# A second planner for the order of each engine: backward by the ends found, forward by the latest times, seven rounds

## The chip, the cores and the metric

The kernel runs on one core of a Trainium2 chip. The metric is the device time of one execution in microseconds. The engines are PE (TensorE, the matmul engine), DVE (VectorE), ACT (ScalarE), POOL (GpSimd) and SP, whose queue issues all DMAs of this kernel.

## What is computed

One inference step of a two-layer streaming encoder for 1152 rows of width 1024 (1024 prompt rows, 8 x 16 sample rows), in float32. The reference, cut to one layer:

```
def _layer(x, l, W, mem_k, mem_v, conv_hist, lat_past, kr_past, start):
    h = _rmsnorm(x, W['norm_mix_g'][l]) @ W['w_in'][l]
    a_u, a_v, b_a, b_g, c_q, c_kv, c_kr = jnp.split(h, cuts, axis=-1)
    y_a, v_rows = _gmlp(a_u, a_v, ...)              # spatial gating in chunks of 128 rows
    y_b, conv_state = _conv_module(b_a, b_g, ...)   # GLU, depthwise convolution of width 31, LayerNorm, swish
    # latent attention: 8 heads, keys and values from a 128-wide latent, QK-norm, rotary part, block-causal mask
    y_c = _mla_attend(q_nope, q_rope, pos, k_nope, kr_all, v, kpos)
    x = x + jnp.concatenate([y_a, y_b, y_c], axis=-1) @ W['w_out'][l]
    # cross-attention into 256 memory tokens, 4 heads of 128, QK-norm
    x = x + om @ W['w_mo'][l]
    x = x + jnp.square(jax.nn.relu(_rmsnorm(x, W['norm_ffn_g'][l]) @ W['w_ff1'][l])) @ W['w_ff2'][l]
```

## The kernel before

The rows lie in three chunks of 384 (`CW`), features on the partitions. Most operands are kept as a high and a low part in fp32r (`halves`, `split`, `split_scaled`), and one product is three matmuls (`mm3`). Two large SBUF areas, `arena_f` (float32) and `arena_r` (fp32r), are cut into buffers by an allocator, and eight PSUM banks are handed round. Weights come by DMA as raw float32, are split by ACT and DVE, and wait in a queue for the matmuls.

A layer runs through five stages: `mixer_in` (input projections; `conv` with 31 passes on DVE for each of two channel tiles, and `taps`, the same convolution for the sample rows as adds on POOL), `attention` (token projections, norms, scores, values) together with `mix` (gating), `mixer_out` (output projection, part of it `early`), `cross`, and `ffn`. In attention each tile of tokens needs a scale: sums of squares on ACT, an add on DVE, a power on POOL (`small_rstd`), then ACT again.

The program is not written in the order in which it runs. Threads (Python generators) emit instructions, and a first planner, `plan`, picks the thread that goes on, by priority and by a model of when each engine is free. This fixes every instruction, its engine, its buffer and its bank, and `log` keeps the planned start of each in `trace`; `real` holds a cost for each (a table of formulas in `mm`, `ptt`, `stt` and the like, as n x 2.1 + 147 ns for an add on POOL). Then `fix_order` works out for each instruction which others it must follow (data, buffers reused, banks reused, order of activation tables), and `in_order` runs a list scheduler over that graph: each engine, and the one DMA queue, takes from what is ready the instruction with the least key. The order that comes out is written into the program as an order for each engine. Between engines `BEHIND` is added: 200 ns after PE, 150 after ACT and DVE, 120 after POOL, 1900 after a DMA. `array` is the planner's model of PE's clock, and `in_order` also charges POOL and DVE for holding one another up.

The key in question is line 420: the planned start, less `URGE` (0.05) times `rest`, the longest chain of costs behind the instruction.

Of the kernel before, what the change touches and what calls it, by code (L numbers as in the profile page):

```python
# [68 lines left out]

TICK = 10240.0 / 3  # L70
WARM = 3060
URGE = 0.05

BEHIND = {"PE": 200.0, "ACT": 150.0, "DVE": 150.0, "POOL": 120.0, "DMA": 1900.0}

# [173 lines left out]
def span(ap, dims, rows):  # L249

    t = ap.tensor
    off, size = ap.offset, sum((n - 1) * abs(s) for s, n in dims) + 1
    if dims[0][0] == math.prod(list(t.shape)[1:]):
        s, n = dims[0]
        size -= (n - 1) * s
        return t.name, off // s, off // s + n, off % s, off % s + size
    if rows:
        s, n = dims[0]
        size -= (n - 1) * s
        return f"{t.name} {off // (s * n)}", 0, 128, off % s, off % s + size  # L260
    return t.name, 0, 128, off, off + size
# [11 lines left out]
class Enc:  # L273
# [39 lines left out]
    def array(self, t, cost, cols):  # L313


        c0 = cols / cost
        if t < self.tick * TICK:
            self.tick, self.cols_out = 0, 0.0
        while True:
            i = int(t // TICK)  # L320
            if i > self.tick:
                self.warm = i == self.tick + 1 and self.cols_out >= WARM
                self.tick, self.cols_out = i, 0.0
            f = 1.0 if self.warm else 2.0
            d = min(cost * f, (i + 1) * TICK - t)
            cost -= d / f
            self.cols_out += c0 * d / f
            if cost < 1e-6:
                return t + d
            t = (i + 1) * TICK + 1e-6  # L330
# [23 lines left out]
    def fix_order(self):  # L354


        n = len(self.trace)
        index = {ins.name: i for i, (_, ins) in enumerate(self.trace)}
        preds = [set() for _ in range(n)]
        for a, b in self.manual:  # L360
            preds[index[a]].add(index[b])
        seen, banks = {}, {b.tensor.name: {} for b in self.banks}
        rows = (self.xscr.tensor.name, self.yscr.tensor.name, self.hscr.tensor.name)
        for i, (_, ins) in enumerate(self.trace):
            new = []
            for write, aps in ((False, ins.ins), (True, ins.outs)):
                for x in aps:
                    ap = getattr(x, "bass_ap", None)
                    if ap is not None and not isinstance(ap.tensor, bass.DRamTensorHandle):
                        new.append((write,) + span(ap, x.ap, ap.tensor.name in rows))  # L370
            for name in {x[1] for x in new if x[1] in banks}:
                used = banks[name]
                preds[i].update(used.values())
                used[ins.engine] = i
            for write, name, p0, p1, lo, hi in new:
                cells = seen.setdefault(name, {})
                for c in range(lo // 128, (hi + 127) // 128):
                    keep = []
                    for e in cells.get(c, ()):
                        j, w, q0, q1, a, b = e  # L380
                        hit = a < hi and lo < b and q0 < p1 and p0 < q1
                        if hit and (w or write) and j != i:
                            preds[i].add(j)
                        a, b = max(a, c * 128), min(b, c * 128 + 128)
                        if not (write and j != i and lo <= a and b <= hi and p0 <= q0 and q1 <= p1):
                            keep.append(e)
                    keep.append((i, write, p0, p1, lo, hi))
                    cells[c] = keep
        prev = {}
        for i in self.in_order(preds):  # L390
            ins = self.trace[i][1]
            if ins.engine in prev:
                self._after(ins, prev[ins.engine])
            prev[ins.engine] = ins
# [9 lines left out]
                k += self.n(ap) > 1  # L404
        return k > 1 or isinstance(ins, mybir.InstTensorCopy)

    def in_order(self, preds):
        n = len(self.trace)
        succ, left, ready = [[] for _ in range(n)], [len(p) for p in preds], [0.0] * n
        for i, p in enumerate(preds):  # L410
            for j in p:
                succ[j].append(i)
        engs = {r[0] for r in self.real}
        rest = [0.0] * n
        for i in reversed(range(n)):
            e = self.real[i][0]
            rest[i] += self.real[i][1]
            for j in preds[i]:
                rest[j] = max(rest[j], rest[i] + (0.0 if e == "PE" == self.real[j][0] else BEHIND[self.real[j][0]]))
        key = [t - URGE * r for (t, _), r in zip(self.trace, rest)]  # L420
        soon, now, free = {e: [] for e in engs}, {e: [] for e in engs}, {e: 0.0 for e in engs}
        columns, narrow, last, out = {}, False, {"DVE": [], "POOL": []}, []
        for i in range(n):
            if not left[i]:
                heapq.heappush(soon[self.real[i][0]], (0.0, i))
        while len(out) < n:
            t, e = min((free[e] if now[e] else max(free[e], soon[e][0][0]), e) for e in engs if now[e] or soon[e])
            while soon[e] and soon[e][0][0] <= t:
                i = heapq.heappop(soon[e])[1]
                heapq.heappush(now[e], (key[i], i))  # L430
            i = None
            if e == "PE" and narrow:
                more = [x for x in now[e] if self.real[x[1]][3]]
                if more:
                    i = min(more)
                    now[e].remove(i)
                    heapq.heapify(now[e])
            _, i = i or heapq.heappop(now[e])
            _, cost, cols, tile = self.real[i]
            if e == "PE":  # L440
                if bool(tile) != narrow:
                    t, narrow = t + 92.0, not narrow
                if tile:
                    cs = range(*tile, 32)
                    t = max([t] + [columns.get(c, 0.0) for c in cs])
                    free[e] = self.array(t, 30.0, cols)
                    end = t + cost * (1.0 if self.warm else 2.0)
                    for c in cs:
                        columns[c] = end
                else:  # L450
                    t = max([t] + list(columns.values()))
                    columns = {}
                    end = free[e] = self.array(t, cost, cols)
            else:
                end = t + cost
                if e == "POOL" or e == "DVE" and self.holds(self.trace[i][1]):
                    for a, b in last["DVE" if e == "POOL" else "POOL"][-12:]:
                        if a <= t < b:
                            end = max(end, b + cost - (60.0 if e == "POOL" else 160.0))
                    last[e].append((t, end))  # L460
                free[e] = end
            out.append(i)
            for j in succ[i]:
                left[j] -= 1
                if e != "PE" or self.real[j][0] != "PE":
                    ready[j] = max(ready[j], end + BEHIND[e])
                if not left[j]:
                    heapq.heappush(soon[self.real[j][0]], (ready[j], j))
        return out

    def _after(self, a, b):
        self.tc.add_manual_dep(
# [33 lines left out]
    def set(self, *name, t=None):  # L506
        self.events[name] = self.last() if t is None else t
# [2351 lines left out]
```

## Time and profile before

| | us |
|---|---|
| median of 3 runs | 3009.69 (3009.36 to 3010.79) |
| the profiled execution | 3009.8 |
| its span, first to last instruction | 3008.0 |
| PE busy | 2920.9 (97%) |
| DVE busy | 2118.2 (70%) |
| ACT busy | 1417.4 (47%) |
| POOL busy | 357.1 (12%) |
| mean granted clock of PE | 0.979 |

Busy time is the union of an engine's instructions. Matmuls overlap, so the mean of one is longer than its share of the busy time. The granted clock is the share of 2.4 GHz that PE was given, as a mean over a stretch; it has two levels, 1.2 and 2.4 GHz. DMAs wait in SP's queue in their order; such waits are told apart from busy time.

### The profile page before, as it was taken

Reading aid. Unit: us, or ns where it says so; the run is one execution under the profiler, and the core shown is the slowest. Engines: PE = TensorE matmul, PEld = TensorE weight load, DVE = VectorE, ACT = ScalarE, POOL = GpSimd, SP = SyncE. Lnnn points to the kernel's source line nnn. Section 1 sums busy time; section 2 is a strip of 40 time slices with the busy share of each in tenths; the row PEclk is TensorE's granted clock in tenths of the full one; section 3 lists DMA queues with packets and bytes.
Section 4 is the critical chain, followed back from the end, with each engine's and each line's share of the span. In section 5 each row is a group of like instructions: output and inputs, shape, how many; then the busy total and the mean of one; then the engine's idle time right before and its main releaser. Section 6 shows DMA issues by size and latency. Waiting matters only on the chain.

```text
span 3008.0 us, 52427 instructions
## 1 busy us (share of the span) xinstructions
PE 2920.9 (97%) x19708; PEld 2807.8 (93%) x19708; DVE 2118.2 (70%) x4568; ACT 1417.4 (47%) x3762; POOL 357.1 (12%) x427
## 2 busy tenths in 40 slices
PE   8989999999999999999999789999999999999999
PEld 8988988979999999999999688989799999999999
DVE  8986767668655577677898867676687555777775
ACT  7566775466544452111364666664665444521110
POOL 0743220000000000000044422120100000000000
PEclk9989998999999999999999889999999999999999
DMA  6302215433232254222333010453333323532221
GB/s 208 113 30 79 66 45 166 153 120 120 101 125 95 106 185 126 90 90 76 111 99 96 26 36 28 136 182 124 123 113 125 110 91 119 181 121 90 90 73 64
DMA packets 156110, 318.14 MB, mean 106 GB/s; under 512 B 22864, under 2 KB 79824, under 8 KB 155600
## 3 DMA queue, kind: packets, MB, share of 16 engines
q1 hardware_dynamic: 155856, 314.79, 31.4%
q8 instruction: 155, 2.54, 0.3%
q14 instruction: 99, 0.81, 0.1%
HBM read 225.94 MB, written 88.80 MB: 105 GB/s over the span
## 4 chain that ended last, share of the span: by engine, by line
PE 87%; DVE 6%; ACT 4%; POOL 1%; issue 1%; DMA 0%; SPq 0%; DVEq 0%; POOLq 0%; ACTq 0%
PE bank L707 84%; PE bank L730 3%; ACT arena_f L589 3%; DVE arena_f L679 1%; POOL arena_f L614 1%; DVE arena_f L610 1%; DVE arena_r L610 1%; DVE arena_f L683 1%; DVE arena_r L679 1%; ACT arena_r L589 1%; ACT L582 0%; DVE arena_r L750 0%; ACT arena_r L606 0%; DVE arena_f L671 0%; DVE bank L691 0%
## 5 line engine op out<-in xcount | busy, mean ns | idle before, releaser
L707 PE MATMUL bank<-arena_r 128*128 128x384 f32 (+7 forms) x16464 | 2671.5, 321 | 38.8 <-DVE arena_r L750 9.3
L707 PEld LDWEIGHTS bank<-arena_r 128*128 128x128 f32 (+2 forms) x16464 | 2539.8, 190 | 103.8 <-ACT arena_f L589 21.2
L610 DVE TENSOR_TENSOR arena_f<-arena_f,bank 128x384 f32<-128x384 f32 (+1 forms) x1286 | 667.3, 529 | 409.9 <-PE bank L707 404.5
L606 ACT CAST arena_r<-arena_f 128x512 fp32r<-128x512 f32 (+5 forms) x547 | 387.8, 729 | 866.9 <-PE bank L707 799.2
L610 DVE TENSOR_TENSOR arena_r<-arena_f,arena_r 128x512 fp32r<-128x512 f32 (+7 forms) x608 | 496.3, 827 | 148.9 <-PE bank L707 124.3
L589 ACT ACTIVATE arena_f<-arena_f 128x384 f32<-128x384 f32 (+5 forms) x628 | 374.8, 620 | 230.0 <-DVE arena_f L610 171.4
L614 POOL TENSOR_TENSOR arena_f<-arena_f 128x128 f32<-128x128 f32 (+6 forms) x298 | 327.3, 1106 | 837.0 <-DVE arena_f L610 284.6
L589 ACT ACTIVATE arena_f<-bank,arena_f 128x64 f32<-128x64 f32 (+7 forms) x774 | 272.6, 424 | 202.1 <-PE bank L707 68.7
L610 DVE TENSOR_TENSOR arena_f<-arena_f 128x384 f32<-128x384 f32 (+11 forms) x832 | 299.0, 371 | 71.5 <-ACT arena_f L589 62.8
L589 ACT ACTIVATE arena_f<-bank 128x64 f32<-128x64 f32 (+6 forms) x682 | 207.7, 349 | 82.6 <-PE bank L707 44.0
L707 PE MATMUL bank<-arena_f 128*128 128x65 f32 (+7 forms) x2344 | 228.4, 290 | 11.1 <-issue 7.9
L679 DVE SCALAR_TENSOR_TENSOR arena_f<-arena_f 128x1024 f32<-128x1024 f32 (+3 forms) x236 | 221.2, 949 | 3.9 <-POOL arena_f L614 1.6
L707 PEld LDWEIGHTS bank<-arena_f 128*128 128x128 f32 (+2 forms) x2344 | 188.1, 158 | 30.7 <-issue 14.0
L730 PE MATMUL bank<-arena_f 128*128 128x128 f32 (+2 forms) x900 | 162.3, 287 | 33.4 <-ACT arena_f L589 23.8
L730 PEld LDWEIGHTS bank<-arena_f 128*128 128x128 f32 (+2 forms) x900 | 111.7, 142 | 61.4 <-ACT arena_f L589 31.4
L695 POOL MEMSET arena_f<- 128x8 f32 (+3 forms) x125 | 30.6, 251 | 973.5 <-DVE arena_r L610 760.7
L606 ACT COPY arena_f<-bank 128x288 f32<-128x288 f32 (+4 forms) x272 | 104.7, 387 | 76.0 <-PE bank L707 62.4
L683 DVE TENSOR_REDUCE arena_f<-bank 128x1 f32<-128x512 f32 (+4 forms) x224 | 119.4, 555 | 10.2 <-PE bank L707 9.5
L589 ACT ACTIVATION_READ_ACCUMULATOR arena_f<-bank 128x1 f32 x396 | 94.1, 275 | 0.0
L610 DVE TENSOR_TENSOR arena_r<-bank,arena_r 128x256 fp32r<-128x256 f32 (+3 forms) x114 | 57.8, 511 | 34.6 <-ACT arena_r L606 33.6
L679 DVE SCALAR_TENSOR_TENSOR arena_r<-bank,arena_f,arena_r 100x512 fp32r<-100x512 f32 (+3 forms) x92 | 65.9, 725 | 17.9 <-ACT arena_r L589 17.2
L589 ACT ACTIVATE arena_r<-bank,arena_f 100x512 fp32r<-100x512 f32 (+3 forms) x92 | 61.7, 690 | 28.6 <-PE bank L730 28.3
(24 smaller groups left out, 538.6 us busy)
## 6 DMA issues: line engine op xcount, KB each, us to landing
arena_f<-w SPq DMA_DIRECT2D x140, 512.0 KB, 3.6
hscr<-arena_f SPq DMA_DIRECT2D x64, 576.0 KB, 3.2
arena_f<-hscr SPq DMA_DIRECT2D x96, 384.0 KB, 3.6
xscr<-arena_f SPq DMA_DIRECT2D x96, 192.0 KB, 1.9
arena_f<-xscr SPq DMA_DIRECT2D x48, 384.0 KB, 4.1
arena_f<-xscr SPq DMA_DIRECT2D x72, 192.0 KB, 2.5
xscr<-arena_f SPq DMA_DIRECT2D x36, 384.0 KB, 2.3
arena_f<-mkc SPq DMA_DIRECT2D x32, 256.0 KB, 3.1
```

What stands on the lines that cost most here:

```text
L589: i = self.nc.scalar.activation(out, in_, func, **kw)
L606: self.nc.scalar.copy(out, in_)
L610: self.nc.vector.tensor_tensor(out=out, in0=a, in1=b, op=op)
L614: self.nc.gpsimd.tensor_tensor(out=out, in0=a, in1=b, op=op)
L679: self.nc.vector.scalar_tensor_tensor(out, a, s, b, op0=o0, op1=o1)
L683: self.nc.vector.tensor_reduce(out, in_, axis=AX.X, op=op, **kw)
L695: self.nc.gpsimd.memset(ap, val)
L707: self.nc.tensor.matmul(out, a, b, start=start, stop=stop, **kw)
L730: self.nc.tensor.transpose(out, in_, self.ident)
```

## The change

`in_order` takes its key from outside, and gives back the order and the modelled end of every instruction. `best_order` calls it seven times. In the first round the key is the planned start alone. After each round `latest` runs a list scheduler backward over the same graph: from the last instruction to the first, each engine takes from what has no unplaced successor the one that ended last in the round before; the negative of the time so found is the latest start, and is the key of the next round. The order with the earliest modelled end of the seven is kept. `URGE` and `rest` go; the backward pass charges the plain costs (30 ns of PE for a matmul on a part of the array), without `array` and without the holding up of POOL and DVE. In `array` two lines go that set the clock model back when time went back; `in_order` now sets it back itself at its start.

```diff
--- before.py
+++ after.py
@@ -69,7 +69,7 @@
 
 TICK = 10240.0 / 3
 WARM = 3060
-URGE = 0.05
+ROUNDS = 7
 
 BEHIND = {"PE": 200.0, "ACT": 150.0, "DVE": 150.0, "POOL": 120.0, "DMA": 1900.0}
 
@@ -314,8 +314,6 @@
 
 
         c0 = cols / cost
-        if t < self.tick * TICK:
-            self.tick, self.cols_out = 0, 0.0
         while True:
             i = int(t // TICK)
             if i > self.tick:
@@ -387,7 +385,7 @@
                     keep.append((i, write, p0, p1, lo, hi))
                     cells[c] = keep
         prev = {}
-        for i in self.in_order(preds):
+        for i in self.best_order(preds):
             ins = self.trace[i][1]
             if ins.engine in prev:
                 self._after(ins, prev[ins.engine])
@@ -404,20 +402,57 @@
                 k += self.n(ap) > 1
         return k > 1 or isinstance(ins, mybir.InstTensorCopy)
 
-    def in_order(self, preds):
+    def best_order(self, preds):
+
+
+        key = [t for t, _ in self.trace]
+        best = None
+        for _ in range(ROUNDS):
+            out, ends = self.in_order(preds, key)
+            if best is None or max(ends) < best[0]:
+                best = max(ends), out
+            key = self.latest(preds, ends)
+        return best[1]
+
+    def latest(self, preds, ends):
         n = len(self.trace)
+        left, ready = [0] * n, [0.0] * n
+        for p in preds:
+            for j in p:
+                left[j] += 1
+        engs = {r[0] for r in self.real}
+        soon, now, free = {e: [] for e in engs}, {e: [] for e in engs}, {e: 0.0 for e in engs}
+        for i in range(n):
+            if not left[i]:
+                heapq.heappush(soon[self.real[i][0]], (0.0, i))
+        start, todo = [0.0] * n, n
+        while todo:
+            t, e = min((free[e] if now[e] else max(free[e], soon[e][0][0]), e) for e in engs if now[e] or soon[e])
+            while soon[e] and soon[e][0][0] <= t:
+                i = heapq.heappop(soon[e])[1]
+                heapq.heappush(now[e], (-ends[i], i))
+            _, i = heapq.heappop(now[e])
+            _, cost, _, tile = self.real[i]
+            free[e] = t + (30.0 if tile else cost)
+            start[i] = -free[e]
+            todo -= 1
+            for j in preds[i]:
+                left[j] -= 1
+                ej = self.real[j][0]
+                ready[j] = max(ready[j], free[e] + (0.0 if e == "PE" == ej else BEHIND[ej]))
+                if not left[j]:
+                    heapq.heappush(soon[ej], (ready[j], j))
+        return start
+
+    def in_order(self, preds, key):
+        n = len(self.trace)
+        self.tick, self.cols_out, self.warm = 0, 0.0, False
+        ends = [0.0] * n
         succ, left, ready = [[] for _ in range(n)], [len(p) for p in preds], [0.0] * n
         for i, p in enumerate(preds):
             for j in p:
                 succ[j].append(i)
         engs = {r[0] for r in self.real}
-        rest = [0.0] * n
-        for i in reversed(range(n)):
-            e = self.real[i][0]
-            rest[i] += self.real[i][1]
-            for j in preds[i]:
-                rest[j] = max(rest[j], rest[i] + (0.0 if e == "PE" == self.real[j][0] else BEHIND[self.real[j][0]]))
-        key = [t - URGE * r for (t, _), r in zip(self.trace, rest)]
         soon, now, free = {e: [] for e in engs}, {e: [] for e in engs}, {e: 0.0 for e in engs}
         columns, narrow, last, out = {}, False, {"DVE": [], "POOL": []}, []
         for i in range(n):
@@ -460,13 +495,14 @@
                     last[e].append((t, end))
                 free[e] = end
             out.append(i)
+            ends[i] = end
             for j in succ[i]:
                 left[j] -= 1
                 if e != "PE" or self.real[j][0] != "PE":
                     ready[j] = max(ready[j], end + BEHIND[e])
                 if not left[j]:
                     heapq.heappush(soon[self.real[j][0]], (ready[j], j))
-        return out
+        return out, ends
 
     def _after(self, a, b):
         self.tc.add_manual_dep(
```

## Rows read from the trace of the kernel before

**Rows 1.** The page, part 1 (whole span), and the core's span and clock

```profile
PE 2920.9 (97%) x19708; PEld 2807.8 (93%) x19708; DVE 2118.2 (70%) x4568; ACT 1417.4 (47%) x3762; POOL 357.1 (12%) x427
...
core 0: 3008.0 us, clock 0.979
```

**Rows 2.** Busy time by stretch (us, then each engine's busy us and count)

```profile
150.00:250.00 100.00, 87.52 (x577) 77.96 (x577) 88.80 (x217) 58.28 (x265) 44.26 (x58) 0.85 0.10 30
250.00:400.00 150.00, 149.06 (x1262) 139.45 (x1261) 104.31 (x366) 109.63 (x494) 38.97 (x54) 1.00 0.23 76
400.00:500.00 100.00, 86.38 (x646) 77.35 (x646) 70.43 (x236) 71.18 (x261) 23.10 (x32) 0.86 0.28 92
500.00:700.00 200.00, 197.43 (x1346) 176.60 (x1346) 124.53 (x274) 105.31 (x250) 10.54 (x10) 0.99 0.42 140
700.00:1550.00 850.00, 849.39 (x5528) 846.31 (x5527) 587.63 (x1039) 325.84 (x527) 14.96 (x18) 1.00 0.34 112
1550.00:1650.00 100.00, 100.00 (x581) 95.87 (x580) 88.78 (x158) 43.49 (x112) 51.68 (x51) 1.00 0.31 95
1650.00:1700.00 50.00, 29.60 (x204) 26.07 (x203) 44.37 (x84) 24.26 (x128) 30.69 (x34) 0.80 0.06 20
1700.00:1900.00 200.00, 182.80 (x1423) 165.38 (x1422) 136.22 (x475) 143.21 (x610) 51.34 (x69) 0.92 0.14 46
1900.00:2000.00 100.00, 96.25 (x725) 90.00 (x724) 71.25 (x234) 60.47 (x238) 21.80 (x29) 0.96 0.51 174
2000.00:2200.00 200.00, 198.31 (x1390) 177.62 (x1390) 128.57 (x293) 114.04 (x268) 11.71 (x13) 1.00 0.34 117
2200.00:3008.00 808.00, 804.07 (x5275) 802.78 (x5273) 532.68 (x940) 266.83 (x412) 0.00 (x0) 1.00 0.32 108
```

**Rows 3.** PE's waits, 1655:1680 (us in total, times, longest)

```profile
PE bank L730 <- ACT arena_f L589: 11.0, 1, 11.0
PE bank L707 <- issue: 7.9, 1, 7.9
```

**Rows 4.** ScalarE's waits, 1650:1700; GpSimd in order of time, 1655:1676

```profile
ACT arena_f L589 <- POOL arena_f L614: 16.7, 13, 5.7
...
1658.35 1.52 POOL L614 TENSOR_TENSOR arena_f<-arena_f 128x128 f32<-128x128 f32 x3
1660.14 15.89 POOL L614 TENSOR_TENSOR arena_f<-arena_f 128x1 f32<-128x1 f32 x12 [0.27 <-DVE arena_f L671]
```

**Rows 5.** Groups by form: GpSimd 1650:1676 (2 rows), VectorE 1600:1700

```profile
L614 POOL TENSOR_TENSOR arena_f<-arena_f 128x128 f32<-128x128 f32 x19 | 19.3, 1017 | 1.3
L614 POOL TENSOR_TENSOR arena_f<-arena_f 128x6 f32<-128x6 f32 x2 | 3.6, 1814 | 0.1
...
L679 DVE SCALAR_TENSOR_TENSOR arena_f<-arena_f 128x1024 f32<-128x1024 f32 x31 | 41.8, 1348 | 0.4
```

**Rows 6.** Groups by form: PE, 1600:1655

```profile
L707 PE MATMUL bank<-arena_r 128*128 128x384 f32 x96 | 18.2, 340 | 0.0
L707 PE MATMUL bank<-arena_r 128*128 128x256 f32 x107 | 14.2, 280 | 0.0
```

**Rows 7.** PE's waits, 1700:2000: the first and last of ten

```profile
PE bank L730 <- ACT arena_f L589: 7.8, 8, 2.0
...
PE bank L730 <- DVE bank L691: 0.2, 1, 0.2
```

**Rows 8.** Groups by form, whole span: GpSimd, VectorE, PE

```profile
L614 POOL TENSOR_TENSOR arena_f<-arena_f 128x6 f32<-128x6 f32 x72 | 101.8, 1420 | 158.7 <-DVE arena_f L610 135.3 <-DVE arena_f L671 11.4 <-ACT arena_r L589 4.4
...
L679 DVE SCALAR_TENSOR_TENSOR arena_f<-arena_f 128x1024 f32<-128x1024 f32 x120 | 158.9, 1324 | 0.9
...
L707 PE MATMUL bank<-arena_f 128*128 128x65 f32 x1152 | 146.5, 275 | 1.0 <-ACT arena_f L589 0.8
```

**Rows 9.** The DMA queue's longest waits; page, part 6: weight loads

```profile
SPq L699 <- DVE arena_f L610: 1109.4, 238, 57.7
...
arena_f<-w SPq DMA_DIRECT2D x140, 512.0 KB, 3.6
```

## The prediction

> **What bounds the kernel now.** I read the totals first [rows 1]. The matmul engine (PE) is busy 2920.9 of 3008.0 us and no other engine passes 70%. So 87 us of idle PE is one pool from which an order can gain. The mean granted clock of 0.979 [rows 1] is the other: a clock that is at 1.2 GHz for a share s of a stretch has the mean 1 - s/2, so 0.979 means that about 4.2% of the span, 126 us, ran at the lower level, at half the speed where PE had work.
>
> The table by stretches shows where both pools lie [rows 2]. The two feed-forward stretches (700 to 1550 and 2200 to 3008 us) are 55% of the span and hold 0.6 + 3.9 us of idle at a clock of 1.00: nothing is to be had there. The reader should look at the rows around them:
> - 150 to 250: idle 12.5, clock 0.85. 400 to 500: idle 13.6, clock 0.86. Between these two, 250 to 400 is full (0.9 idle, 1.00).
> - 1550 to 1650 is full (0.0 idle). Then 1650 to 1700: idle 20.4, clock 0.80; 1700 to 1900: idle 17.2, 0.92; 1900 to 2000: idle 3.8, 0.96.
> - What is left of the 87, about 10 us, falls before 150 us, by subtraction; the start has nothing ready to be put in order, and I leave it out.
>
> The lost clock in a stretch is about its length times (1 - clock) times PE's busy share: 13 (150 to 250), 12 (400 to 500), 6 (1650 to 1700), 15 (1700 to 1900), 4 (1900 to 2000), in all 50 us. With the idle time of these five stretches, 67 us, the ceiling for any order of the same work is **117 us**. It is a ceiling, not a forecast: some of it is dependency.
>
> The worst hole shows that not all is. Between 1655 and 1675 PE stands 7.9 us, then 11.0 us [rows 3]. What ends the second wait is ScalarE, and ScalarE waited 16.7 us for GpSimd in that stretch [rows 4]. GpSimd worked without a gap from 1660.1 to 1676.0 [rows 4], and what it worked at was mostly the short convolution's taps for the sample rows: 19 adds of 1.017 us, with two of the power operations of 1.8 us among them [rows 5]. Those few power operations give the token scales for attention, on which the next PE work hangs; the taps are wanted only at the end of mixing. VectorE did the same: 31 convolution passes of 1.35 us from 1600 to 1700 [rows 5]. And just before the hole PE had run 18.2 + 14.2 us of matmuls of 384 and 256 columns [rows 6]. By the code these are gating projections for the most part (some of the 256 belong to tokens of attention): some 30 us that could have filled the hole. Filler burnt early and a short urgent operation behind long patient ones: that is what a key made of planned times does.
>
> **The change, part by part.** No instruction is added or removed; the engines, DMA queue, buffers and banks of each stay as the first planner gave them, and with them every write-after-read edge. Only the order on each engine and on the DMA queue changes.
>
> *The key.* Before, it is the planned time less 5% of the longest chain behind the operation (line 420). After, the first round uses the planned time alone, and each later round the latest time at which an operation may start so that what follows can still end in time, with each engine treated as one server. In the 1655 hole the taps and convolution passes have late deadlines, the power operations early ones. Credit, stretch by stretch, from the idle and clock losses above:
> 1. 1650 to 1700 (20.4 + 6 = 26): the filler of 30 us in [rows 6] covers the two stands of 18.9, but waking the chain earlier has its own latency. I take two thirds, 17.
> 2. 150 to 250 (12.5 + 13 = 25.5): the same stage of layer 0, with waits of several sources and DVE busy 88.8 of 100 [rows 2]. One third, 8.5.
> 3. 400 to 500 (13.6 + 12 = 25.6): the end of attention, just behind a stretch of 150 us in which PE never lacked work. Urgent chains could be run in that stretch and the patient work kept. One third, 8.5.
> 4. 1700 to 2000 (21 + 19 = 40): 32 waits, none over 2.0 us, spread over ten pairs of line and releaser [rows 7]. One quarter, 10.
>
> Sum 44 us. The thirds and the quarter are judgement; the ends are nothing and all, 0 and 117.
>
> *What is pushed back.* Convolution passes are 120 in all, 158.9 us [rows 8]. Moved out of the opening of attention they land in 250 to 400 and 1700 to 2000, where VectorE has 45.7 of 150 and 92.5 of 300 us free [rows 2]: about half of the 79 us of a layer fits under that cover. Without cover, a pass of 1.32 us stands ahead of a PSUM read and PE waits for its bank. If one pass in eleven does this, 11 x 1.3 = 14 us come back, which I charge. Ends: 0 (cover holds) and 60 (half the passes of one layer and a quarter of the other's, 45 x 1.32).
>
> *GpSimd's price in the backward pass.* The backward pass charges a tap 128 x 2.1 + 147 = 416 ns and knows nothing of VectorE. The trace has 1.017 us in the hole and 1.52/3 = 0.51 us for a run of three at 1658.35 [rows 4, 5]. So the latest times of what stands ahead of taps are up to 0.6 us each too late, some 10 taps deep: at most 6 us of the 17 of item 1. The Trainium skill has a rule here (GPSIMD Engine Reference, Key points): GpSimd shares its SBUF interfaces with VectorE, which collides with VectorE instructions that read two SBUF inputs. By it, pulling the convolution passes away from the taps would itself quicken the taps; at 0.51 instead of 1.017 ten taps would give 5 us more. The trace has both durations, but cannot tell whether the convolution pass is the cause, so neither 5 nor 6 is in the sum.
>
> *The clock in the backward pass.* It knows no clock; the forward pass does and judges the rounds. Price nothing by itself; it belongs to the second rival.
>
> *DMA order.* Loads are put in order of need too. The queue is in order and already stands 1109.4 us in 238 waits on one line of VectorE, up to 57.7 at once, while weight loads land in 3.6 us [rows 9]; the feed-forward stretches show that this costs PE nothing now. Taken at 0; if a weight load comes late, its cover is gone and PE waits about 3.6 us plus a split of some 2 us. Ends: -2 and +20 (three or four such loads).
>
> *The choice among seven, the two lines of the clock model that go, and the resets.* They run on the host. The first planner's PE time never goes back, so the removed lines did nothing there; 0. The old order is not among the seven, so nothing guards against an order worse than the old.
>
> Sum: -44 + 14 = **-30 us**. The profiled execution took 3009.8 us (span 3008.0), 0.1 above the median of 3009.69; 3009.8 - 30 = **2980 us**.
>
> **The rivals.**
> *Nothing moves (3004 to 3016).* The planned end comes earlier and the chip's does not: buffers and write-after-read edges stay, so the filler may not be free to move, and gain and loss cancel. For it: 55% of the span cannot change, and the sparse waits of 1700 to 2000 have many sources. Against it: the filler in [rows 6] depends only on normed rows that were there long before. Price: within 6 us, some 3010.
>
> *Tight order, many small waits (slower, about 3031).* PE's queue is in order. An order that puts each urgent matmul where the planner thinks its operand comes stalls PE whenever it comes later, while patient work stands behind. The planner is off: a power operation of six columns is charged 1.29 us and takes 1.42, a convolution pass 1.19 against 1.32, and the 65-column value matmuls 222 ns against 127 [rows 8], 0.11 ms too much over 1152 of them, so from attention on its clock is far from the chip's. Price: in 1700 to 2000 such waits cost 21 us of idle and 19 of clock in 300 us, 0.13 us per us. In the stretches now full (250 to 400, 500 to 700, 1550 to 1650, 2000 to 2200: 650 us) the same density would cost 87 us, three quarters of it 65; less the 44 gained, +21: 3031. It decides from half that density (44 us) upward. Against it: the old order comes from the same charges and has only 0.9 us of idle in 250 to 400. The Trainium skill puts a rule beside this (TensorE: Matmul & The Clock Gate, A second HAM failure mode: psum-queue depth-cycling): frequent micro-idles between groups of matmuls make the clock fall and rise, and throughput goes with it. By that rule, the trace agrees: the clock is 0.92 in 1700 to 1900, where no wait passes 2.0 us [rows 2, 7].
>
> *A late load in a feed-forward stretch (slower, 3018 to 3030).* The DMA end above with no gain beside it.
>
> **How the numbers follow.** The forecast has 0.60, with its own range 2945 to 3003: its low end is 65 of the 117, more than half of everything. Nothing moves: 0.13. Tight order: 0.22; late loads: 0.05. A measurement of this kernel can tell about 0.2% (6 us) from no change, so faster is 0.60, same 0.13, slower 0.27. The range must reach into the tight order until two tenths are left out: 2938 to 3033.
>
> **What would show it.** Right: the hole at 1655 to 1675 shrinks to under 6 us, taps and convolution passes reach past 1700 us, gating projections (256 and 384 columns) appear among attention's matmuls, PE idle falls from 87 to about 60 us and the mean clock rises from 0.979 to 0.985 or more, while both feed-forward stretches keep their lengths. Wrong: idle of over 5 us in a stretch now full, a longer list of sub-microsecond waits of PE for VectorE or ScalarE with a clock under 0.979, or idle in the feed-forward stretches ended by a weight load or its split.

## The result, and the profile after

| | before | after |
|---|---|---|
| median, us | 3010.24 (3009.36 to 3016.2, 4 runs) | 2955.78 (2954.61 to 2961.57, 4 runs) |
| the profiled execution, us | 3009.8 | 2961.57 |
| its span, us | 3008.0 | 2959.7 |

The ratio is 0.9819, with a 95% interval of 0.9801 to 0.9837: 54 us faster by the medians. The profiled execution of after is the longest of its four, so the profile shows 48 of the 54.

The totals of after and the core's clock, to be read against [rows 1]:

```profile
PE 2896.2 (98%) x19708; PEld 2793.5 (94%) x19708; DVE 2115.3 (71%) x4568; ACT 1415.2 (48%) x3762; POOL 355.1 (12%) x427
...
core 0: 2959.7 us, clock 0.988
```

PE's busy time fell by 24.7 us and its idle time from 87.1 to 63.5, by 23.6. The matmuls are the same 19708, so the busy time that went is clock: the mean rose from 0.979 to 0.988. One less the mean, times the span, is 63 us before and 36 after, which at a busy share of 97 to 98% gives some 27 us, as far as three digits of the clock tell. Both pools of the prediction gave, in about equal parts.

The stretches of after (span; then busy us and count of PE, PE's weight loads, DVE, ACT, POOL; granted clock; DMA share; GB/s), against [rows 2]. Later stages begin earlier here, so a row does not cover quite the same work:

```profile
150.00:250.00 100.00, 93.14 (x716) 86.20 (x715) 87.59 (x227) 65.33 (x286) 42.19 (x63) 0.95 0.11 36
250.00:400.00 150.00, 149.51 (x1263) 142.67 (x1262) 111.70 (x380) 109.97 (x496) 40.30 (x54) 1.00 0.24 77
400.00:500.00 100.00, 89.50 (x742) 78.80 (x741) 70.06 (x230) 72.30 (x264) 20.99 (x28) 0.93 0.34 115
500.00:700.00 200.00, 199.01 (x1258) 180.49 (x1258) 141.21 (x301) 109.84 (x253) 9.06 (x9) 1.00 0.44 147
700.00:1550.00 850.00, 850.00 (x5508) 844.95 (x5507) 589.96 (x1018) 319.60 (x509) 32.24 (x33) 1.00 0.33 109
1550.00:1650.00 100.00, 83.50 (x510) 81.00 (x509) 87.23 (x161) 46.80 (x171) 58.52 (x61) 0.91 0.28 79
1650.00:1700.00 50.00, 48.18 (x379) 44.29 (x377) 44.85 (x137) 38.41 (x158) 13.42 (x16) 1.00 0.09 29
1700.00:1900.00 200.00, 189.95 (x1598) 173.98 (x1599) 142.69 (x486) 141.17 (x564) 50.63 (x73) 0.97 0.19 63
1900.00:2000.00 100.00, 98.60 (x734) 93.96 (x733) 64.63 (x205) 58.29 (x237) 18.57 (x20) 0.93 0.59 198
2000.00:2200.00 200.00, 199.81 (x1263) 180.01 (x1262) 147.59 (x312) 117.26 (x265) 10.36 (x9) 1.00 0.35 117
2200.00:2959.70 759.70, 755.75 (x4985) 755.11 (x4983) 488.24 (x854) 241.53 (x358) 0.00 (x0) 1.00 0.32 105
```

The end of layer 0's attention (400 to 500) now idles 10.5 us instead of 13.6 at a clock of 0.93 instead of 0.86; 1700 to 1900 idles 10.1 instead of 17.2 at 0.97 instead of 0.92. The feed-forward rows are full as before. But 1550 to 1650, full before, now has 16.5 us of idle: the large hole of layer 1 has not gone, it came earlier.

To compare equal work, I take the starts of certain matmuls in both traces: the first with 416 columns (token projections), the first with 65 (values of attention) and the first with 288 (feed-forward) of each layer.

| from, to | before, us | after, us | gained |
|---|---|---|---|
| start to token projections of layer 0 | 88.0 | 88.3 | -0.3 |
| to its first value matmul | 136.4 | 125.9 | 10.5 |
| to its feed-forward | 515.4 | 499.9 | 15.5 |
| to the token projections of layer 1 | 838.6 | 837.4 | 1.2 |
| to its first value matmul | 128.6 | 124.6 | 4.0 |
| to its feed-forward | 535.1 | 517.7 | 17.4 |
| to the end | 765.9 | 765.9 | 0.0 |

### The profile page after: what moved, and what is told of

It reads as the page before. It is cut to its first block, busy times and chain, and to the rows that moved or that the text cites. A ratio compares the mean times of both kernels' runs of the same rounds, so it can differ in the third digit from the quotient of the medians.

```text
span 2959.7 us, 52473 instructions
## 1 busy us (share of the span) xinstructions
PE 2896.2 (98%) x19708; PEld 2793.5 (94%) x19708; DVE 2115.3 (71%) x4568; ACT 1415.2 (48%) x3762; POOL 355.1 (12%) x427
## 4 chain that ended last, share of the span: by engine, by line
PE 87%; DVE 6%; ACT 4%; POOL 1%; issue 1%; DMA 0%; SPq 0%; DVEq 0%; POOLq 0%; ACTq 0%
PE bank L743 85%; ACT arena_f L625 3%; PE bank L766 3%; DVE arena_f L715 2%; DVE arena_f L646 1%; DVE arena_r L646 1%; POOL arena_f L650 1%; DVE arena_f L719 1%; ACT arena_r L625 1%; DVE arena_r L715 1%; DVE arena_r L786 0%; DVE arena_f L707 0%; DVE bank L727 0%; ACT arena_f L642 0%; ACT L618 0%
## 5 line engine op out<-in xcount | busy, mean ns | idle before, releaser
L650 POOL TENSOR_TENSOR arena_f<-arena_f 128x128 f32<-128x128 f32 (+7 forms) x298 | 325.1, 1096 | 777.3 <-DVE arena_f L707 277.2
L625 ACT ACTIVATE arena_f<-bank,arena_f 128x64 f32<-128x64 f32 (+7 forms) x774 | 278.8, 428 | 178.8 <-PE bank L743 60.9
L646 DVE TENSOR_TENSOR arena_f<-arena_f 128x32 f32<-128x32 f32 (+10 forms) x832 | 296.5, 368 | 57.8 <-ACT arena_f L625 48.5
L743 PEld LDWEIGHTS bank<-arena_f 128*128 128x128 f32 (+2 forms) x2344 | 189.7, 157 | 26.7 <-issue 12.7
L715 DVE SCALAR_TENSOR_TENSOR arena_r<-bank,arena_f,arena_r 100x512 fp32r<-100x512 f32 (+3 forms) x92 | 65.8, 724 | 16.0 <-ACT arena_r L625 15.5
```

What stands on the lines that cost most here:

```text
L625: i = self.nc.scalar.activation(out, in_, func, **kw)
L646: self.nc.vector.tensor_tensor(out=out, in0=a, in1=b, op=op)
L650: self.nc.gpsimd.tensor_tensor(out=out, in0=a, in1=b, op=op)
L715: self.nc.vector.scalar_tensor_tensor(out, a, s, b, op0=o0, op1=o1)
L743: self.nc.tensor.matmul(out, a, b, start=start, stop=stop, **kw)
```

## The hole that stayed

PE's waits in 1550 to 1650 of after (total, times, longest), against [rows 3]:

```profile
PE bank L766 <- ACT arena_f L625: 9.6, 1, 9.6
PE bank L743 <- issue: 6.5, 1, 6.5
```

ScalarE's longest wait in 1600 to 1650, and the taps on POOL (1610 to 1640) and convolution passes on DVE (1550 to 1650), against [rows 4, 5]:

```profile
ACT arena_f L625 <- POOL arena_f L650: 21.7, 19, 5.8
```

```profile
L650 POOL TENSOR_TENSOR arena_f<-arena_f 128x128 f32<-128x128 f32 x24 | 25.8, 1073 | 1.8
...
L715 DVE SCALAR_TENSOR_TENSOR arena_f<-arena_f 128x1024 f32<-128x1024 f32 x34 | 46.6, 1370 | 0.2
```

The picture is that of before: PE stands 6.5 and 9.6 us, ScalarE waits 21.7 us for POOL, POOL runs taps at 1.07 us each. An order by latest times should not leave taps in front of attention's tokens unless the tokens cannot go without them. They can't: in the graph of edges of this program, attention's first tiles of tokens in layer 1 have 57 to 60 of the layer's 60 taps before them. The path is three steps long: a tap reads its product from scratch (words 2115 to 2243 of the float32 area, say); ScalarE then writes the squares of a token tile over that scratch; the add and the power on POOL need the squares. The write must follow the tap. It is an edge from the way scratch was handed out, and no order can cross it. The first plan, its costs and this graph are the same before and after the change.

The filler did not move either. PE in 1580 to 1630 of after, against [rows 6]:

```profile
L743 PE MATMUL bank<-arena_r 128*128 128x384 f32 x96 | 18.2, 340 | 0.0
```

The same 96 matmuls of 384 columns run before the hole, for the same 18.2 us. PE was full there in before (100.00 of 100 us, [rows 2]), and the list scheduler takes the least key among what is ready: filler kept back would have left PE idle earlier, unless something else was ready. This last step is argued from the code; no run keeps the filler back.

## The experiments

The planner's own end for an order, which it works out when the program is made, is no time of the chip, but it is what the choice among rounds goes by, and I give it where it bears on the result:

```
                       planned end   measured median, us
before                 2978.6        3010.2 to 3014.1 (four sets of runs)
plan_key  (round 1)    2986.2        3025.5
two_rounds             2933.0        2974.7
three_rounds           2923.5        2971.9
after (seven rounds)   2912.6        2955.8
nine_rounds            2911.9        2959.2
tap_scratch_l1         2899.4        2946.8
```

### How many rounds: plan_key, two_rounds, three_rounds, nine_rounds

The edit of plan_key; the other three have 2, 3 and 9:

```diff
-ROUNDS = 7
+ROUNDS = 1
```

> One round only: the key is the planned time alone, no backward pass, and the 5% of the longest chain is gone. Theory A (the latest times from the backward pass make the gain): as before or worse, 3005 to 3030 us, with PE idle of 85 us or more and holes at 200, 430 and 1660 us as before. Rival B (the 5% of the longest chain was what hurt, and leaving it out is the gain): 2955 to 2970 us.

> Two rounds: one backward pass, one choice. Theory A: a first set of latest times brings most of the gain, 2960 to 2985 us. Rival C (it is the search that counts: seven tries and the best kept): less than half of the 54 us, 2985 to 3010 us.

> Three rounds: the third order is kept, whose planned end lies 11 us after that of the order that seven rounds keep. If the chip follows the planned end even in such steps: 2962 to 2972 us. If below some 20 us the planned end says nothing of the chip: anything from 2950 to 2980 us, and not in the place that the planned end gives it.

> Nine rounds: another order is kept, with a planned end only 0.7 us before that of seven rounds. If the planned end tells the chip's time: 2952 to 2960 us, like seven rounds. The distance from 2956 shows how far two orders of one planned end lie apart on the chip; 10 us or more would mean that choices between rounds are partly chance.

Measured: plan_key 3025.5 us (ratio 1.0052, 1.0037 to 1.0067), two_rounds 2974.7 (0.9880, 0.9863 to 0.9896), three_rounds 2971.9 (0.9860, 0.9845 to 0.9875), nine_rounds 2959.2 (0.9819, 0.9804 to 0.9833).

Theory A stands and rival B falls: without the 5% of the chain the kernel is 15 us slower, so that term was worth something and its loss is no part of the gain. The first backward pass brings 51 us from there, 36 against before: two thirds of the whole. The search adds 19. The last third thus belongs to rival C. Steps of 10.9 us and more in the planned end come back on the chip in the right order, though not in their size (three_rounds was expected at 2962 to 2972 and came at 2971.9, at the edge). The 9.5 us between two and three rounds came as 3, and the intervals of the two overlap; 0.7 us of planned end does not come back, seven and nine rounds being 3 us apart the other way, inside what was expected.

### Whose order: pe_alone, side_engines, dma_old

Each finds the round that would be kept, and then makes one more order in which only some engines use that round's key; the others use the key of before (rest, worked out as there, is the longest chain behind each instruction). NEW is ("PE",), then ("ACT", "DVE", "POOL"), then all four engines without the DMA queue:

```diff
-                best = max(ends), out
+                best = max(ends), key
             key = self.latest(preds, ends)
-        return best[1]
...
+        return self.in_order(preds, [k if r[0] in NEW else t - 0.05 * q
+            for k, r, (t, _), q in zip(best[1], self.real, self.trace, rest)])[0]
```

> PE takes the key of the round that was kept; ACT, DVE, POOL and the DMA queue keep the key of the kernel before (planned time less 5% of the chain). Theory A1 (the gain is PE keeping filler back): 2960 to 2985 us. Rival D (the gain is short urgent work passed ahead on ACT, DVE and POOL): 3000 to 3015 us.

> ACT, DVE and POOL take the key of the round that was kept; PE and the DMA queue keep the key of the kernel before. Theory A1: little, 2995 to 3012 us. Rival D: most of the gain, 2958 to 2980 us. If both this and the run with PE alone give about half, the two orders add up.

> All four engines take the key of the round that was kept; the DMA queue alone keeps the key of the kernel before. If the order of the loads is worth nothing, as the prediction took it: within 6 us of the changed kernel, 2950 to 2962 us. If loads in order of need carry part of the gain: 2965 to 2990 us.

Measured: pe_alone 2999.7 us (ratio 0.9959, 0.9944 to 0.9975), side_engines 2997.0 (0.9954, 0.9939 to 0.9969), dma_old 2973.9 (0.9878, 0.9863 to 0.9892). Against the 3010.8 and 3011.1 of their own runs of before: 11, 14 and 37 us faster.

Theory A1 falls: PE's order alone gives a fifth of the gain. Rival D falls too: so do the side engines alone. Together with PE they give 37, more than 11 + 14. My reading is that PE can only keep work for a chain that the other engines then let through; the runs show that the orders depend on one another, and not that this is why. The stretches of pe_alone:

```profile
150.00:250.00 100.00, 93.21 (x632) 85.53 (x630) 86.70 (x225) 60.81 (x273) 50.21 (x64) 0.86 0.10 30
400.00:500.00 100.00, 85.91 (x667) 77.00 (x667) 71.04 (x238) 72.77 (x265) 24.57 (x33) 0.91 0.30 96
1650.00:1700.00 50.00, 29.54 (x208) 26.39 (x207) 44.73 (x88) 24.93 (x135) 31.06 (x32) 0.80 0.07 20
```

and of side_engines:

```profile
150.00:250.00 100.00, 86.70 (x618) 78.46 (x617) 88.76 (x220) 60.58 (x270) 46.43 (x61) 0.90 0.11 33
400.00:500.00 100.00, 88.60 (x698) 79.66 (x697) 71.67 (x242) 72.38 (x266) 24.99 (x33) 0.91 0.26 84
1650.00:1700.00 50.00, 28.56 (x191) 24.47 (x189) 44.28 (x88) 23.28 (x126) 29.34 (x31) 0.76 0.04 13
```

With PE alone, 150 to 250 idles 6.8 us instead of 12.5, but 400 to 500 still 14.1; with the side engines alone it is the other way, 13.3 and 11.4. At 1650 to 1700 both idle over 20, as before.

The prediction took the order of the loads at 0. Taking the new one away costs what is left: dma_old is 18 us behind the changed kernel, three times what the expectation left for "nothing". The planner foresees most of it, with an end of 2926.3 for this order against 2912.6; three_rounds, whose planned end is 2923.5, took 2971.9, so dma_old took what an order of such an end takes. Two reservations: the scheduler follows what is ready, so a different DMA order also shifts the order on the engines, and the run does not hold that still; and which load or store does it is not settled. In the two profiles (spans of 2972.2 and 2959.7 us) 9 of the 12.5 us lie in layer 1 before its feed-forward (128.8 and 522.5 us where after has 124.6 and 517.7), not in the feed-forward where most weights are loaded.

### The scratch edge: tap_scratch, tap_scratch_before, tap_scratch_l1

The first two give the taps 256 words of their own out of the general area, in the changed kernel and in the kernel before:

```diff
         self.SM, self.smp = F.alloc(256), 0
+        tp = F.alloc(256)
+        self.TP = Arena(self, F.ap, tp.lo, tp.lo + tp.n, "P")
...
-                p = self.tmp(128)
+                p = self.TP.alloc(128)
```

The third takes them in layer 1 alone, for as long as its convolution runs:

```diff
         acc = []
+        if l:
+            tp = yield from self.A(F, 256)
+            self.TP = Arena(self, F.ap, tp.lo, tp.lo + tp.n, "P")
...
-                p = self.tmp(128)
+                p = (self.TP if l else self.TF).alloc(128)
...
             zt.free()
+        if l:
+            tp.free()
```

> The changed kernel, with 256 words taken from the general float32 area as scratch of their own for the products of the short convolution (taps) on the sample rows, so that the squares of attention's tokens are no longer written over scratch that a tap must first have read. Theory E (the hole at 1629 to 1645 us that the change left is this edge, not the order): the hole shrinks under 6 us, 10 to 18 us less idle PE in 1550 to 1700 and some in 150 to 250, time 2930 to 2948 us. Rival F (the hole is GpSimd's own queue, slowed by VectorE, or the length of the chain): the hole stays, 2950 to 2962 us; smaller general area may also cost a few us.

> The same scratch in the kernel before, with its own key. Theory E with the order as a second condition: without the latest times the freed edge is hardly used, 3000 to 3010 us. If the edge alone made the hole: 2985 to 3000 us.

> The changed kernel with scratch of their own for the taps' products in layer 1 alone, 256 words of the general area while the convolution runs; layer 0 keeps the shared scratch. With scratch in both layers the hole of layer 1 closed and layer 1 up to its feed-forward was 14 us shorter, while layer 0 lost 7. If the 14 come from the freed edge and the 7 from the smaller area in layer 0: 2938 to 2947 us, clearly under the changed kernel. If what one layer gains and the other loses is the chance of another order: 2950 to 2962 us.

Measured: tap_scratch 2953.1 us (2949.55 to 2959.43; ratio 0.9807, 0.9789 to 0.9825), tap_scratch_before 3015.2 (1.0009, 1.0000 to 1.0019), tap_scratch_l1 2946.8 (2943.1 to 2949.39; 0.9773, 0.9757 to 0.9789).

The stretch 1600 to 1650 of the changed kernel, and then 150 to 250, 1600 to 1650 and 1650 to 1700 of tap_scratch:

```profile
1600.00:1650.00 50.00, 33.69 (x236) 32.35 (x236) 48.08 (x65) 22.39 (x100) 38.98 (x41) 0.83 0.23 70
```

```profile
150.00:250.00 100.00, 88.80 (x634) 82.51 (x634) 87.36 (x221) 67.44 (x347) 48.18 (x63) 0.93 0.17 52
1600.00:1650.00 50.00, 50.00 (x376) 48.98 (x375) 44.37 (x101) 29.13 (x115) 28.62 (x43) 1.00 0.18 50
1650.00:1700.00 50.00, 40.53 (x282) 34.39 (x280) 43.60 (x130) 29.48 (x138) 16.59 (x17) 0.90 0.10 32
```

The hole is gone: 33.69 us of PE became 50.00, the clock 0.83 became 1.00. Theory E stands on this row, rival F falls. The time of the whole does not say so, 2953.1 against 2955.8 with overlapping intervals: 150 to 250 idles 11.2 us where after had 6.9, 9.5 us of idle stand after 1650, and by the same first matmuls as above layer 1 is 14 us shorter up to its feed-forward (628.4 against 642.3) while layer 0 is 7 longer (721.4 against 714.1). The changed areas make another first plan, and 256 words fewer for all else. The expectation was missed on both counts: idle PE in 1550 to 1700 fell by 9 us (18.3 to 9.5) where 10 to 18 were expected, and 2953.1 lies above 2930 to 2948. No run changes the areas and leaves the edge, so a part of the effect may be the new plan; but the hole went in all three versions.

tap_scratch_before, 1650 to 1700 (the hole of before, [rows 2]), 1700 to 1750 and the last feed-forward:

```profile
1650.00:1700.00 50.00, 49.02 (x384) 46.99 (x382) 44.15 (x100) 29.76 (x133) 26.40 (x32) 1.00 0.13 37
1700.00:1750.00 50.00, 38.95 (x269) 32.68 (x269) 41.42 (x129) 24.70 (x95) 11.10 (x11) 0.90 0.07 24
2240.00:3012.00 772.00, 763.79 (x5008) 762.00 (x5006) 491.70 (x861) 242.89 (x363) 0.00 (x0) 1.00 0.32 104
```

The edge made the hole: with the old key too, PE is busy 49.02 of 50 where it was busy 29.60. My second condition, that the latest times are needed to use the freed edge, was wrong, and so was the rival's time: the idle comes back elsewhere (11.1 us in 1700 to 1750; 8.2 us in the last feed-forward, which is 9 us longer), and the whole is no faster. By the same first matmuls layer 1 is 13 us shorter up to its feed-forward here too (651.1 against 663.7), and what it gains is lost in layer 0 (5 us) and the two feed-forwards (2 and 9).

tap_scratch_l1 keeps 13 of the 14 us in layer 1 (629.0 against 642.3) and avoids the 7 in layer 0 (714.4 against 714.1):

```profile
1600.00:1650.00 50.00, 47.78 (x351) 46.14 (x351) 41.37 (x93) 30.95 (x134) 33.36 (x41) 0.97 0.18 54
1650.00:1700.00 50.00, 43.77 (x315) 38.63 (x314) 44.48 (x134) 29.84 (x118) 13.72 (x17) 0.90 0.12 39
```

On POOL the powers of the tokens now run among the taps. From 1610 to 1650 there are four of six columns beside 21 taps, where after had 24 taps and no such power from 1610 to 1640:

```profile
L650 POOL TENSOR_TENSOR arena_f<-arena_f 128x6 f32<-128x6 f32 x4 | 6.8, 1711 | 1.2 <-DVE arena_f L646 1.0
```

It came at the far end of the 2938 to 2947 expected, 9 us under the changed kernel by the medians. The two ran beside different runs of before, so the ratios tell it better: 0.9773 (0.9757 to 0.9789) against 0.9819 (0.9801 to 0.9837). This version beats both kernels.

### One wrong charge mended: value_cost, value_cost_three

```diff
-            real = max(n / 0.6, 216.0) + 6.0
+            real = 112.0 if n == 65 else max(n / 0.6, 216.0) + 6.0
```

with seven rounds, and with three.

> The changed kernel with one charge mended: a value matmul of 65 columns costs 112 ns in both passes instead of 222; in the trace such matmuls start 112 ns apart. If the wrong charge misplaced work in attention (the prediction's second rival put weight on it): 2940 to 2950 us. If order is forgiving of a wrong charge: 2950 to 2962 us.

> The mended charge of 112 ns for a value matmul, with three rounds: another order under the same charges. With seven rounds the mended charge came out 26 us slower than the old charge. If the lower charge itself does harm (work of attention counts as less urgent than it is): 2970 to 2990 us again. If that was the chance of one order: nearer to three rounds with the old charge, 2955 to 2970 us.

Measured: value_cost 2981.6 us (ratio 0.9898, 0.9882 to 0.9915), value_cost_three 2983.7 (0.9899, 0.9885 to 0.9914). The trace of after bears the mended charge out (148.8 us for 1152 of them is 129 ns at most, against 222):

```profile
L743 PE MATMUL bank<-arena_f 128*128 128x65 f32 x1152 | 148.8, 273 | 0.9 <-ACT arena_f L625 0.6 <-DVE arena_f L646 0.2
```

and yet the orders made with it are slower on the chip: with seven rounds by 26 us (2981.6 against 2955.8, outside both expectations), with three by 12 (2983.7 against three_rounds' 2971.9). Two orders of two are slower, with intervals that do not touch, so the chance of a single order is an unlikely cause; two are few. value_cost in 250 to 400, 400 to 500 and 1700 to 1800, and then 1700 to 1800 of after:

```profile
250.00:400.00 150.00, 147.02 (x1234) 139.56 (x1233) 112.37 (x378) 109.02 (x496) 38.87 (x52) 1.00 0.24 77
400.00:500.00 100.00, 87.32 (x728) 77.71 (x728) 66.27 (x223) 71.48 (x264) 20.90 (x28) 0.91 0.31 100
1700.00:1800.00 100.00, 88.25 (x668) 75.85 (x667) 73.31 (x259) 72.70 (x335) 29.64 (x40) 0.93 0.11 35
```

```profile
1700.00:1800.00 100.00, 92.86 (x734) 82.27 (x735) 77.08 (x279) 76.69 (x354) 32.38 (x44) 0.97 0.12 39
```

PE is short of work in more places of attention (3.0 us of idle in 250 to 400, where after has 0.5; 12.7 in 400 to 500 against 10.5; 11.8 in 1700 to 1800 against 7.1). A charge that is too high makes PE's work in attention look longer, and what it hangs on more urgent; it may act as a reserve against the delays that the planner does not see. That was not tried (a charge over 222 would tell), and it stays open.

## Why the prediction was right, and where it was not

The sign, the place and the two pools were right: the gain lies between the token projections and the feed-forward of both layers, half as idle time and half as clock, and the feed-forward kept its lengths (837.4 for 838.6, 765.9 for 765.9). The time was inside the range of 95 us, but the gain was 54 where 30 was forecast, and of the terms only one was about the right size. By the table of equal work item 1 was 13 too high, items 2 to 4 together 16 too low, and the charge of 14 did not come; that these leave a sum of the right order is in part luck.

Of the signs named beforehand, idle PE (63.5, about 60 forecast), the clock (0.988) and the feed-forward came. Three did not: the hole did not shrink under 6 us, taps and convolution passes do not reach past 1700 us, and 96 gating matmuls still run before the hole, as in before. A sign of being wrong came too, over 5 us of idle in a stretch that was full: 16.5 in 1550 to 1650, which is the old hole begun earlier.

- **Item 1** (the hole of layer 1, 17 us): 4.0. The step that failed is "the power operations have early deadlines and the taps late ones". I read the queue of POOL and took the order for the cause; the taps had early deadlines, through scratch that the tokens reuse. The filler that was to cover the stands was not kept back. The doubt stood only in the first rival, by which write-after-read edges stay. With the edge freed, layer 1 up to its feed-forward is 13 to 14 us shorter.
- **Item 2** (layer 0's opening, 8.5): 10.5. About right.
- **Item 3** (the end of layer 0's attention, 8.5): 15.5 over the whole stage to the feed-forward. The share was too small; the shares were judgement, as the text said. Of the 15.5, pe_alone has 0.2, side_engines 4.8 and dma_old 13.8, by the same first matmuls. That fits urgent chains run early and patient work kept, but no run shows that it was this.
- **Item 4** (small waits of layer 1, 10): 17.4 to the feed-forward. PE's waits in 1700 to 2000 fell from 20.7 us in 32 [rows 7] to 11.8 in 25; the first of ten rows was 7.8 in 8 and is

```profile
PE bank L766 <- ACT arena_f L625: 2.7, 4, 1.1
```

- **Passes pushed back** (+14): nothing that the rows show. In layer 0 some did go back: from 240 to 300 us there are 13, where before had 5, and PE idles 0.5 us in 250 to 400, so the cover held. In layer 1 they stayed: 34 of them stand in 1550 to 1650, as 31 did in 1600 to 1700. The edge of item 1 does not tie them all: in the graph attention's first tiles have 30 of the layer's 60 passes before them. The rest may have run because DVE had little else while the tokens waited for the taps; that is not tested. This charge and item 1 (13 too much) nearly cancelled.

```profile
L679 DVE SCALAR_TENSOR_TENSOR arena_f<-arena_f 128x1024 f32<-128x1024 f32 x5 | 6.1, 1229 | 0.0
...
L715 DVE SCALAR_TENSOR_TENSOR arena_f<-arena_f 128x1024 f32<-128x1024 f32 x13 | 16.6, 1274 | 0.1
```

- **DMA order** (0, bounds -2 and +20): the run with the old DMA key puts it at about -18. I argued from the feed-forward, where the queue's waits cost nothing, and gave the gain no room; by the profiles most of it lies before the feed-forward of layer 1. Without these 18 the gain would be 37.
- **The choice among seven** was taken as a matter for the host. It is worth 19 of the 54 (two_rounds against seven). This and the DMA order are the largest misses among the terms taken at 0; they are no further parts of the sum, but cut the same gain another way.
- **Tight order** did not come. It rested on prices read as the mean duration of one instruction. Such instructions overlap: in the trace of after, an operation of another kind that follows a convolution pass without a wait starts 1.196 us after the pass did (median of 86), where the pass lasts 1.28 (its median) and the planner charges 1.195; powers of six columns in a row start 1.287 apart (median of 9), and are charged 1.288. There the planner was right where I called it off. It was not where one pass follows another: of 24 such pairs none starts under 1.30 us apart, and the median is 1.40. For the value matmuls it is off too, and there the wrong charge does no harm. The rule of the Trainium skill beside this rival (TensorE: Matmul & The Clock Gate, A second HAM failure mode: psum-queue depth-cycling) agrees in direction: from 1700 to 2000, with 11.5 us of idle instead of 20.9, the clock is 0.95 instead of 0.93. Stretch by stretch it does not hold: 1700 to 1900 went from 0.92 to 0.97, but 1900 to 2000 from 0.96 to 0.93 with less idle.
- **POOL's price in the backward pass**: the taps ran no faster in the hole of the changed kernel (1.073 us against 1.017), where the passes had not moved. In tap_scratch_l1, from 1610 to 1650, with 10 convolution passes in 40 us where after has 17 in 30, they did:

```profile
L650 POOL TENSOR_TENSOR arena_f<-arena_f 128x128 f32<-128x128 f32 x21 | 13.7, 655 | 8.8 <-ACT arena_f L625 8.1
...
L715 DVE SCALAR_TENSOR_TENSOR arena_f<-arena_f 128x1024 f32<-128x1024 f32 x10 | 12.9, 1291 | 0.0
```

0.655 us a tap against 1.073. That agrees in direction with the Trainium skill (GPSIMD Engine Reference, Key points), by which VectorE instructions with two SBUF inputs collide with GpSimd; no run here parts the passes from the rest of what DVE did.

## What to carry to other kernels

Before an order is blamed for a short operation that stands behind long patient ones, follow its edges: scratch handed out again can tie it to them, and then no order helps, but another buffer can. Latest times from a backward pass over the whole schedule were worth two thirds of the gain in a single pass, and here they had to go to all queues together, the DMA queue too: PE alone, or the side engines alone, gave a fifth and a quarter of it. Price an instruction in a queue by the distance of starts, not by its duration, and by what follows it (1.20 or 1.40 us for the same pass); and try a mended charge on the chip before it is believed.

## What the runs showed of the hardware

Durations on ACT and DVE overlap more than I had expected: an activation of 64 columns from PSUM with a scale lasts 326 ns, and the instruction that follows it without a wait starts 196 ns after it did (medians of 341 in after). A convolution pass that follows another does not overlap it: the 24 such pairs start 1.40 us apart. And the clock is half of what this order is worth: of the 48 us that the two profiles differ by, 24.7 are busy time of the same matmuls.
